# Differential attention's scores on one Trainium2 core: from 128-row products per map to pairs of 64-row products in one four-bank tile

## The chip, the cores and the metric

The kernel runs on one core of one Trainium2 chip. The metric is the device time of one execution in microseconds. Before the change it is 2376.85 us, the median of three runs (2373.96 to 2377.68).

## The reference

A two-layer decoder trunk on x of 1024 tokens by 1024 channels, float32. Layer 0 mixes tokens with gated linear attention, layer 1 with differential attention; each mixer is followed by a SwiGLU, with RMS norms ahead and residual sums behind. The change is in the differential attention alone, whose core is:

```
lam = exp(sum(lam_q1 * lam_k1)) - exp(sum(lam_q2 * lam_k2)) + lambda_init
for blk in range(S // Q_BLOCK):
    s = einsum('bhcqd,bhckd->bhcqk', qb, kb) * scale
    s = where(kpos[None, :] <= qpos[:, None], s, -inf)
    p = softmax(s, axis=-1)
    a = p[:, :, 0] - lam * p[:, :, 1]
    outs.append(einsum('bhqk,bhkv->bhqv', a, vb))
```

There are 8 heads, two maps per head (index c), 64 channels per map, and blocks of 128 query rows. Values have 128 channels per head.

## The kernel before, in words

Activations lie transposed, channels on the partitions, tokens in two halves of 512. Products run with operands in the format fp32r, and an fp32 number is split into a rounded high part and a low part; `mm3` (lines 145 to 148) makes one exact product of three: high by high, high by low, low by high. All projections and both SwiGLU layers use it.

The attention stage is in the second half of `trunk_kernel`, from line 1127 on. For a head n and a half s of the queries, `qstep` and `kstep` project 128 channels (two maps of 64) into a PSUM bank of pool A and split the result. To get by with two products per score bank, they lay the parts so that the contraction has 128 rows: for map m, `kk` holds the high part of K in rows 0 to 63 and the low part in rows 64 to 127; `qh` holds the high part of Q twice, in both halves; `ql` holds the low part of Q in rows 0 to 63, and zeros, written once by POOL, in rows 64 to 127.

`scores(i)` (lines 1196 to 1225) treats the 128 query rows of chunk i, whose score width is W = 128 (i + 1) columns, that is one bank of up to 512 columns for i below 4 and two for i of 4 to 7. For each map it takes a tile of two banks from pool S (two such tiles), makes the products

```
mm(out, qh[:, o:o + P], kk[:, :w], start=True, stop=False)
mm(out, qlo[:, o:o + P], kk[:, :w], start=False, stop=True)
```

then adds the causal mask to the last 128 columns on VectorE (line 1210), takes the negated row maximum (1212), exponentiates on ScalarE with that maximum as bias and the row sum as second result (1215), inverts the sum (1217), and for map 1 multiplies it by minus lambda (1219). Two more VectorE passes scale the first map's rows and add the second's (1223, 1224). `values(i)` transposes the weights by 128 x 128 blocks (1235), copies them back (1236) and multiplies by the values (1240); `dnorm` normalizes a half of a head.

PSUM has eight banks: two tiles of two for scores, one for the outputs (O), one for transposes and norms (C), two for projections (A). A table of blocks, 16 halves of heads, sets what stands beside what: `merge` lays the projections of later heads and the output projection (`dout_steps`) between the chunks of a half. From this the tile framework's scheduler makes the order of each engine; the engines then run that order strictly, waiting on each other through semaphores.

## Time and profile before

| what | value |
| --- | --- |
| median of three runs | 2376.85 us |
| profiled execution, own time | 2377.06 us |
| profiled execution, span from first to last instruction | 2375.3 us |
| PE (products) busy | 2321.8 us, 98% |
| PEld (weight loads, beside PE) busy | 1934.6 us, 81% |
| DVE (VectorE) busy | 1827.5 us, 77% |
| ACT (ScalarE) busy | 1078.4 us, 45% |
| POOL (GpSimd) busy | 191.3 us, 8% |
| mean granted clock of TensorE | 0.996 |

The products overlap in the pipeline and their recorded ends are modelled, so the busy time of PE is no measure of its rate: what a product costs in a stream is read from the distance between two starts. A product of fp32 operands (transposes and values) shows as two records. The first score product starts at 1166.8 us, the last at 1675.2 us from the span's start.

### The profile page before, as it was taken

The numbers are of one execution on the slowest core, as the hardware profiler recorded it, in microseconds if no ns is written. First come the engines' busy times: TensorE is split into PE (matmuls) and PEld (weight loads), VectorE is DVE, ScalarE is ACT, GpSimd is POOL, SyncE is SP. The second block draws the span as 40 slices with busy tenths as digits, with TensorE's granted clock in tenths as the row PEclk, the third lists the DMA queues.
The fourth block names the chain that finished last, engine by engine and source line by source line (L and its number), as shares of the span: only waits on it lengthen the run. The fifth ranks groups of instructions, "written<-read, shape, count | busy, mean of one in ns | idle before, by whom it ended". The sixth has DMA issues, their size and how long they took to land. (4 is left out here: it accounts for less than half of the span.)

```text
span 2375.3 us, 30798 instructions
## 1 busy us (share of the span) xinstructions
PE 2321.8 (98%) x11682; PEld 1934.6 (81%) x11682; DVE 1827.5 (77%) x3039; ACT 1078.4 (45%) x1741; POOL 191.3 (8%) x194
## 2 busy tenths in 40 slices
PE   8999999999999999999999999999999999999997
PEld 7888888888888887887888878887788888887876
DVE  6988676898666667988877785868996666669887
ACT  6555554544333334334565454646543333334344
POOL 4000000000000000442000000000000000002443
PEclk9999999999999999999999999999999999999999
DMA  5121222113233336442010101110113332246332
GB/s 193 45 89 54 89 80 80 55 50 111 94 101 113 114 99 217 144 158 93 32 36 19 36 19 36 36 36 15 48 58 117 109 107 93 94 160 211 121 123 87
DMA packets 82871, 212.15 MB, mean 89 GB/s; under 512 B 9249, under 2 KB 11425, under 8 KB 82722
## 3 DMA queue, kind: packets, MB, share of 16 engines
q1 hardware_dynamic: 82434, 210.02, 26.9%
q8 instruction: 92, 1.51, 0.3%
q14 instruction: 57, 0.47, 0.1%
q10 hardware_dynamic: 288, 0.16, 0.0%
HBM read 167.14 MB, written 42.99 MB: 88 GB/s over the span
## 5 line engine op out<-in xcount | busy, mean ns | idle before, releaser
L881 POOL TENSOR_TENSOR sums<-wraw 128x256 f32<-128x256 f32 x36 | 29.2, 810 | 2100.0 <-DMA wraw<-in_foutc 1083.5
L935 DVE TENSOR_TENSOR x<-x,psB 128x512 f32<-128x512 f32 (+1 forms) x246 | 162.6, 669 | 31.5 <-PE psB L933 31.1
L142 DVE TENSOR_TENSOR w0l<-wraw,w0h 128x1024 fp32r<-128x1024 f32 (+2 forms) x60 | 68.2, 1136 | 98.9 <-ACT w0h L141 98.9
L1215 ACT ACTIVATE p<-sp,mx 128x128 f32<-128x128 f32 (+7 forms) x128 | 94.5, 741 | 82.1 <-DVE mx L1212 79.0
L740 PE MATMUL psB<-hl,w0h 128*128 128x512 f32 x320 | 124.5, 389 | 0.0
L739 PE MATMUL psB<-hh,w0h 128*128 128x512 f32 x320 | 124.5, 389 | 0.0
L741 PE MATMUL psB<-hh,w0l 128*128 128x512 f32 x320 | 124.5, 389 | 0.0
L141 ACT CAST w0h<-wraw 128x1024 fp32r<-128x1024 f32 (+2 forms) x60 | 58.9, 982 | 134.0 <-PE psB L740 112.1
L141 ACT CAST w2h<-wraw 128x1024 fp32r<-128x1024 f32 (+2 forms) x58 | 56.8, 980 | 116.9 <-PE psB L740 86.8
L142 DVE TENSOR_TENSOR w3h<-wraw,w3h 128x512 fp32r<-128x512 f32 x40 | 27.6, 691 | 97.7 <-ACT w3h L141 97.7
L223 DVE TENSOR_TENSOR x<-x,psA 128x512 f32<-128x512 f32 x108 | 73.4, 683 | 33.0 <-PE psA L148 31.5
L1212 DVE TENSOR_REDUCE mx<-sp 128x1 f32<-128x128 f32 (+7 forms) x128 | 94.5, 750 | 1.4
L141 ACT CAST w3h<-wraw 128x512 fp32r<-128x512 f32 x42 | 26.1, 620 | 132.0 <-DMA wraw<-in_fin 131.9
L1240 PE MATMUL psO<-aT,vd 128*128 128x128 f32 x576 | 82.1, 281 | 1.6 <-ACT aT L1236 1.4
L1240 PEld LDWEIGHTS psO<-aT,vd 128*128 128x128 f32 x576 | 72.3, 192 | 12.8 <-ACT aT L1236 11.1
L1207 PE MATMUL sp<-kk,qh 128*128 128x512 f32 (+2 forms) x192 | 69.5, 366 | 2.6 <-ACT p L1215 1.8
L740 PEld LDWEIGHTS psB<-hl,w0h 128*128 128x128 f32 x320 | 60.1, 188 | 12.5
L739 PEld LDWEIGHTS psB<-hh,w0h 128*128 128x128 f32 x320 | 60.1, 188 | 12.5
L741 PEld LDWEIGHTS psB<-hh,w0l 128*128 128x128 f32 x320 | 60.1, 188 | 12.4
L141 ACT CAST w1h<-wraw 128x1024 fp32r<-128x1024 f32 (+1 forms) x44 | 45.5, 1035 | 51.9 <-DVE wraw L711 40.7
L142 DVE TENSOR_TENSOR w2l<-wraw,w2h 128x1024 fp32r<-128x1024 f32 (+2 forms) x58 | 66.7, 1150 | 0.3
L142 DVE TENSOR_TENSOR w1l<-wraw,w1h 128x1024 fp32r<-128x1024 f32 (+1 forms) x44 | 52.8, 1200 | 17.6 <-ACT w1h L141 16.7
(737 smaller groups left out, 7774.6 us busy)
## 6 DMA issues: line engine op xcount, KB each, us to landing
wraw<-in_fin SPq DMA_DIRECT2D x88, 512.0 KB, 3.6
stash<-e SPq DMA_DIRECT2D x108, 256.0 KB, 4.0
hl<-stash SPq DMA_DIRECT2D x80, 256.0 KB, 4.4
wraw<-in_foutc SPq DMA_DIRECT2D x40, 512.0 KB, 3.6
wraw<-in_gin SPq DMA_DIRECT2D x32, 512.0 KB, 3.5
stash<-raw SPq DMA_DIRECT2D x40, 256.0 KB, 4.0
wraw<-in_gv SPq DMA_DIRECT2D x16, 512.0 KB, 3.6
wraw<-in_gout SPq DMA_DIRECT2D x16, 512.0 KB, 3.5
```

The source lines that it names most:

```text
L141: ins = nc.scalar.copy(out=hi, in_=src)
L142: nc.vector.tensor_tensor(out=lo, in0=src, in1=hi.bitcast(F32), op=ALU.subtract)
L223: nc.vector.tensor_tensor(out=xt[m][s], in0=xt[m][s], in1=ps, op=ALU.add)
L739: mm(ps, ah, bh, start=s, stop=False, skip_group_check=cont)
L740: mm(ps, ah, bl, start=False, stop=False, skip_group_check=cont)
L741: mm(ps, al, bh, start=False, stop=i == KH - 1, skip_group_check=cont)
L881: op(out=s1, in0=a21, in1=a22, op=ALU.add)
L935: tt(out=xt[i + o][s][:, c], in0=xt[i + o][s][:, c], in1=ps, op=ALU.add)
L1207: mm(out, qh[:, o:o + P], kk[:, :w], start=True, stop=False)
L1212: nc.vector.reduce_max(out=mx, in_=sp[:, :W], axis=AX.X, negate=True)
L1215: nc.scalar.activation(out=p[:, :W], in_=sp[:, :W], func=AF.Exp, bias=mx, accum_out=sm)
L1240: mm(c["op"][:, o:o + P], tl["v", n // 2][:, j, v * P:(v + 1) * P], aT[:, j * P:(j + 1) * P], start=j == 0, stop=j == i)
```

## The change

Q and K are split once for both maps, with 128 rows each: rows 0 to 63 are map 0, rows 64 to 127 map 1. A score bank is made of three products of 64 rows per map (high by high, high by low, low by high), issued as pairs, map 0 and map 1 one behind the other, each map into its own two banks of a tile of four banks; pool S has one such tile. The products of a chunk are kept in program order and given a higher priority. Scores are made with the sign turned round, so that mask and row minimum are one VectorE instruction over the whole width, which writes the masked scores back; the exponential turns the sign. The row sums of both maps lie in one tile of two columns, inverted together and multiplied by (1, minus lambda) together. The tile p1 gets a second buffer. The output projection of the last heads takes its four borrowed banks from the one tile. The core of the diff:

```diff
-        psum(pc, ("S", 2), ("O", 1), ("C", 1), ("A", 2))
-        ql = [[ap.tile([P, HT], F32R, name=f"ql{i}_{m}") for m in range(2)] for i in range(2)]
-        for i in range(2):
-            for m in range(2):
-                nc.gpsimd.memset(ql[i][m][64:128, :].bitcast(F32), 0.0)
+        psum(pc, ("S", 1), ("O", 1), ("C", 1), ("A", 2))
-        scale = 64 ** -0.5
+        scale = -64 ** -0.5
+        cmask = ap.tile([P, S], F32, name="cmask")
+        nc.gpsimd.memset(cmask, 0.0)
+        nc.gpsimd.affine_select(out=cmask[:, S - P:], in_=cmask[:, S - P:], pattern=[[-1, P]], base=0,
+                                channel_multiplier=1, compare_op=ALU.is_ge, fill=1e30)
...
-                for m in range(2):
-                    src = ps[64 * m:64 * m + 64, :]
-                    hi = ap.tile([P, HT], F32R, name=f"qh{m}", bufs=2)
-                    nc.scalar.mul(hi[0:64, :], src, scale)
-                    nc.scalar.mul(hi[64:128, :], src, scale)
-                    nc.vector.scalar_tensor_tensor(out=ql[s][m][0:64, :], in0=src, scalar=scale,
-                                                   in1=hi[0:64, :].bitcast(F32), op0=ALU.mult, op1=ALU.subtract)
+                hi, lo = [ap.tile([P, HT], F32R, name=f"q{x}", bufs=2) for x in "hl"]
+                nc.scalar.mul(hi, ps, scale)
+                nc.vector.scalar_tensor_tensor(out=lo, in0=ps, scalar=scale, in1=hi.bitcast(F32), op0=ALU.mult,
+                                               op1=ALU.subtract)
...
-                for m in range(2):
-                    src = ps[64 * m:64 * m + 64, :]
-                    kk = ap.tile([P, HT], F32R, name=f"kk{m}", bufs=3)
-                    nc.scalar.copy(out=kk[0:64, :], in_=src)
-                    nc.vector.tensor_tensor(out=kk[64:128, :], in0=src, in1=kk[0:64, :].bitcast(F32),
-                                            op=ALU.subtract)
+                hi, lo = [ap.tile([P, HT], F32R, name=f"k{x}", bufs=3) for x in "hl"]
+                split(hi, lo, ps)
...
-                for m in range(2):
-                    qh, qlo = tl["q", n, s, m]
-                    sp = PS["S"].tile([P, S], F32, name="sp")
+                both = PS["S"].tile([P, 2 * S], F32, name="sp")
+                sps = both[:, :S], both[:, S:]
+                rows = slice(0, 64), slice(64, 128)
+                with tc.high_priority(200):
                     for b in range((W + HT - 1) // HT):
                         w = min(HT, W - b * HT)
-                        kk = tl["k", n, b, m]
-                        out = sp[:, b * HT:b * HT + w]
-                        mm(out, qh[:, o:o + P], kk[:, :w], start=True, stop=False)
-                        mm(out, qlo[:, o:o + P], kk[:, :w], start=False, stop=True)
-                    diag = sp[:, W - P:W]
-                    nc.vector.tensor_tensor(out=diag, in0=diag, in1=cmask, op=ALU.add)
+                        kh, klo = tl["k", n, b]
+                        for x, (q, k) in enumerate(((qh, kh), (qh, klo), (qlo, kh))):
+                            for m in range(2):
+                                ins = mm(sps[m][:, b * HT:b * HT + w], q[rows[m], o:o + P], k[rows[m], :w],
+                                         start=x == 0, stop=x == 2)
+                                if (b, x, m) != (0, 0, 0):
+                                    tc.keep_in_program_order(ins)
+                for m in range(2):
+                    sp = sps[m]
                     mx = ap.tile([P, 1], F32, name="mx", bufs=4)
-                    nc.vector.reduce_max(out=mx, in_=sp[:, :W], axis=AX.X, negate=True)
-                    p = ap.tile([P, S], F32, name=f"p{m}", bufs=2 - m)
-                    sm = ap.tile([P, 1], F32, name="sm", bufs=6)
-                    nc.scalar.activation(out=p[:, :W], in_=sp[:, :W], func=AF.Exp, bias=mx,
-                                         accum_out=sm)
-                    nc.vector.reciprocal(out=sm, in_=sm)
-                    if m == 1:
-                        nc.vector.tensor_tensor(out=sm, in0=sm, in1=neglam, op=ALU.mult)
+                    nc.vector.tensor_tensor_reduce(out=sp[:, :W], in0=sp[:, :W], in1=cmask[:, S - W:], scale=1.0,
+                                                   scalar=1e30, op0=ALU.add, op1=ALU.min, accum_out=mx)
+                    p = ap.tile([P, S], F32, name=f"p{m}", bufs=2)
+                    nc.scalar.activation(out=p[:, :W], in_=sp[:, :W], func=AF.Exp, scale=-1.0, bias=mx,
+                                         accum_out=sm[:, m:m + 1])
+                nc.vector.reciprocal(out=sm, in_=sm)
+                nc.vector.tensor_tensor(out=sm, in0=lam, in1=sm, op=ALU.mult)
```

Since the change also moves instructions, three places of the order follow. In it "x2" means two instructions of one line in a row. Line 1205 of the change is the score product, 1234 and 1239 are the transposes and value products (1235 and 1240 before), 144 to 146 the projections (146 to 148 before).

PE, the chunk of 768 columns (i = 5) of a head in the middle of the stage; before:

```order
L1235 MATMUL psC<-ident,p_11430 128x128 x4
L1207 MATMUL sp<-kk_10834,qh_11070 128x512
L1208 MATMUL sp<-kk_10834,ql_0_9631 128x512
L1207 MATMUL sp<-kk_11147,qh_11070 128x256
L1208 MATMUL sp<-kk_11147,ql_0_9631 128x256
L1207 MATMUL sp<-kk_10837,qh_11074 128x512
L1208 MATMUL sp<-kk_10837,ql_1_9632 128x512
L1207 MATMUL sp<-kk_11150,qh_11074 128x256
L1240 MATMUL psO<-aT,vd 128x128 x4
L1208 MATMUL sp<-kk_11150,ql_1_9632 128x256
```

and with the change, in the next head:

```order
L145 MATMUL psA<-hl_0_9522,w3h 128x512
L1205 MATMUL sp<-kh,qh 128x512 x2
L1205 MATMUL sp<-kl,qh 128x512 x2
L1205 MATMUL sp<-kh,ql 128x512 x2
L1205 MATMUL sp<-kh,qh 128x256 x2
L1205 MATMUL sp<-kl,qh 128x256 x2
L1205 MATMUL sp<-kh,ql 128x256 x2
L166 MATMUL psC<-sq,onesr 128x512
```

Eight score products, into which value products were mixed, have become twelve of half the rows, in six pairs without a break. So it is in 60 of the 64 chunks; in four of the 128-column chunks one to four projections stand between the first pair and the other two.

PE, the end of the stage, from the last score products of head 7's second half (1024 columns) to the first chunks of its first half (128 and 256 columns); before:

```order
L1208 MATMUL sp<-kk_14390,ql_1_9632 128x512
L147 MATMUL psA<-dol_14500,w3h 128x512
L148 MATMUL psA<-doh_14499,w3l 128x512
L1235 MATMUL psC<-ident,p_14554 128x128 x4
L1207 MATMUL sp<-kk_14356,qh_14661 128x128
L1208 MATMUL sp<-kk_14356,ql_0_9629 128x128
L146 MATMUL psA<-doh_14499,w3h 128x512
L1235 MATMUL psC<-ident,p_14554 128x128 x3
L1240 MATMUL psO<-aT,vd 128x128 x7
L147 MATMUL psA<-dol_14500,w3h 128x512
L148 MATMUL psA<-doh_14499,w3l 128x512
L1207 MATMUL sp<-kk_14359,qh_14665 128x128
```

and with the change:

```order
L1205 MATMUL sp<-kh,qh 128x512 x2
L1205 MATMUL sp<-kl,qh 128x512 x2
L1205 MATMUL sp<-kh,ql 128x512 x2
L1234 MATMUL psC<-ident,p_14349 128x128 x7
L1239 MATMUL psO<-aT,vd 128x128 x7
L1205 MATMUL sp<-kh,qh 128x128 x2
L1205 MATMUL sp<-kl,qh 128x128 x2
L1205 MATMUL sp<-kh,ql 128x128 x2
L1234 MATMUL psC<-ident,p_14392 128x128 x7
L1205 MATMUL sp<-kh,qh 128x256 x2
L1205 MATMUL sp<-kl,qh 128x256 x2
L1205 MATMUL sp<-kh,ql 128x256 x2
```

Between the chunk of 1024 columns and the first one of 128 stood two projections and four transposes, with the second map's products for later; now seven transposes and seven value products stand there, and both maps' products follow together.

DVE, the chunk of 1024 columns in head 1 (line 223 before, 221 now, adds the output projection to x); before:

```order
L1210 TENSOR_TENSOR sp<-sp,cmask 128x128
L1212 TENSOR_REDUCE mx<-sp 128x1
L1210 TENSOR_TENSOR sp<-sp,cmask 128x128
L223 TENSOR_TENSOR x_0_82<-x_0_82,psA 128x512
L1212 TENSOR_REDUCE mx<-sp 128x1
L1217 RECIPROCAL sm<-sm 128x1
L223 TENSOR_TENSOR x_0_84<-x_0_84,psA 128x512
L1223 TENSOR_SCALAR p_10944<-p_10944,sm 128x1024
L1217 RECIPROCAL sm<-sm 128x1
L1219 TENSOR_TENSOR sm<-sm,neglam 128x1
L1224 SCALAR_TENSOR_TENSOR p_10944<-p_10956,sm,p_10944 128x1024
```

and with the change, where line 1213 is the new wide instruction and, as "mx", its small second one:

```order
L1213 ISA sp,mx<-sp,cmask 128x1024
L1213 ISA mx 128x1
L221 TENSOR_TENSOR x_0_79<-x_0_79,psA 128x512
L221 TENSOR_TENSOR x_0_81<-x_0_81,psA 128x512
L1213 ISA sp,mx<-sp,cmask 128x1024
L1213 ISA mx 128x1
L1219 RECIPROCAL sm<-sm 128x2
L1220 TENSOR_TENSOR sm<-lam,sm 128x2
L1222 TENSOR_SCALAR p_10884<-p_10884,sm 128x1024
L1223 SCALAR_TENSOR_TENSOR p_10884<-p_10888,sm,p_10884 128x1024
```

Two mask additions, two reductions, two reciprocals and one multiplication have become two wide and two small instructions, one reciprocal and one multiplication, with two x additions between the two maps.

## Rows read from the trace of the kernel before

**Rows 1.** The page, busy time and instructions by engine; granted clock in 40 slices.

```profile
PE 2321.8 (98%) x11682; PEld 1934.6 (81%) x11682; DVE 1827.5 (77%) x3039; ACT 1078.4 (45%) x1741; POOL 191.3 (8%) x194
...
PEclk9999999999999999999999999999999999999999
```

**Rows 2.** Two stretches: length; busy us of PE, PEld, DVE, ACT, POOL; PE's clock.

```profile
1165.00:1700.00 535.00, 518.99 (x3018) 434.43 (x3017) 405.50 (x838) 299.63 (x602) 0.00 (x0) 1.00 0.10 31
...
1650.00:1700.00 50.00, 42.29 (x212) 32.43 (x211) 44.49 (x93) 30.59 (x63) 0.00 (x0) 0.97 0.13 43
```

**Rows 3.** Who waited for whom, 1165:1700: us, times, longest.

```profile
PEld sp L1207 <- ACT p L1215: 7.7, 20, 0.8
PE sp L1207 <- ACT p L1215: 1.8, 4, 0.6
```

**Rows 4.** PE in order of time, score products: start us, length us, line, shape.

```profile
1317.06 0.34 PE L1208 MATMUL sp<-kk,ql 128*128 128x384 f32 x1
1317.23 0.34 PE L1207 MATMUL sp<-kk,qh 128*128 128x384 f32 x1
...
1331.84 0.39 PE L1208 MATMUL sp<-kk,ql 128*128 128x512 f32 x1
1332.07 0.22 PE L1207 MATMUL sp<-kk,qh 128*128 128x128 f32 x1
1332.13 0.27 PE L1208 MATMUL sp<-kk,ql 128*128 128x128 f32 x1
1332.24 0.45 PE L1207 MATMUL sp<-kk,qh 128*128 128x512 f32 x1
1332.53 0.39 PE L1208 MATMUL sp<-kk,ql 128*128 128x512 f32 x1
...
1564.67 0.28 PE L1207 MATMUL sp<-kk,qh 128*128 128x256 f32 x1
1564.79 0.28 PE L1208 MATMUL sp<-kk,ql 128*128 128x256 f32 x1
```

**Rows 5.** PE in order of time, around a block of line 481.

```profile
220.59 0.39 PE L148 MATMUL psA<-hh,w1l 128*128 128x512 f32 x1
220.91 0.68 PE L481 MATMUL psB<-u 128*64 128x64 f32 x8
221.52 0.50 PE L146 MATMUL psA<-oh,w2h 128*128 128x512 f32 x1
221.85 0.40 PE L147 MATMUL psA<-ol,w2h 128*128 128x512 f32 x1
```

**Rows 6.** Weight loads (PEld) in order of time, same stretch.

```profile
220.37 0.19 PEld L148 LDWEIGHTS psA<-hh,w1l 128*128 128x128 f32 x1
220.91 0.54 PEld L481 LDWEIGHTS psB<-u 128*64 128x64 f32 x8 [0.35 <-issue]
...
221.62 0.19 PEld L147 LDWEIGHTS psA<-ol,w2h 128*128 128x128 f32 x1
```

**Rows 7.** Groups by shape, 1165:1690, 1024-wide minimum pass and exponential: busy, mean ns, idle.

```profile
L1212 DVE TENSOR_REDUCE mx<-sp 128x1 f32<-128x1024 f32 x16 | 19.5, 1218 | 0.3
...
L1215 ACT ACTIVATE p<-sp,mx 128x1024 f32<-128x1024 f32 x16 | 17.9, 1117 | 16.9 <-DVE mx L1212 15.7 <-DVE sm L1217 1.2
```

**Rows 8.** PE in order of time, a run of value products.

```profile
1658.44 1.73 PE L1240 MATMUL psO<-aT,vd 128*128 128x128 f32 x14
```

**Rows 9.** Groups by line over the span, DVE in the attention: count, busy us, mean ns.

```profile
L1210 DVE TENSOR_TENSOR sp<-sp,cmask 128x128 f32<-128x128 f32 x128 | 36.7, 293 | 30.2 <-PE sp L1208 29.5
L1166 DVE TENSOR_TENSOR kk<-psA,kk 64x512 fp32r<-64x512 f32 x32 | 22.1, 689 | 8.0 <-ACT kk L1165 7.1
L1153 DVE SCALAR_TENSOR_TENSOR ql<-psA,qh 64x512 fp32r<-64x512 f32 x32 | 21.9, 685 | 9.4 <-ACT qh L1152 8.3
L1217 DVE RECIPROCAL sm<-sm 128x1 f32<-128x1 f32 x128 | 19.8, 159 | 12.5 <-ACT p L1215 11.5
```

**Rows 10.** Groups by shape, DVE, 1650:1700.

```profile
L1210 DVE TENSOR_TENSOR sp<-sp,cmask 128x128 f32<-128x128 f32 x10 | 2.9, 288 | 0.2 <-PE sp L1208 0.2
```

More of the change, by code (lines that the diff above doesn't have):

```diff
@@ L68, in trunk_kernel @@
     onesr = const.tile([P, P], F32R, name="onesr")
-    cmask = const.tile([P, P], F32, name="cmask")
+    lam = const.tile([P, 2], F32, name="lam")
     vec = const.tile([P, 48], F32, name="vec")
-    neglam = const.tile([P, 1], F32, name="neglam")
     gdiff = const.tile([P, 1], F32, name="gdiff")
@@ L89, in trunk_kernel @@
                             compare_op=ALU.is_equal, fill=0.0)
-    nc.vector.memset(cmask, 0.0)
-    nc.gpsimd.affine_select(out=cmask, in_=cmask, pattern=[[-1, P]], base=0, channel_multiplier=1,
-                            compare_op=ALU.is_ge, fill=-1e30)
     dots = const.tile([P, 2], F32, name="dots")
@@ L103, in lam_consts @@
         nc.scalar.activation(out=dots, in_=dots, func=AF.Exp)
+        neglam = lam[:, 1:2]
+        nc.vector.memset(lam, 1.0)
         nc.vector.tensor_tensor(out=neglam, in0=dots[:, 1:2], in1=dots[:, 0:1], op=ALU.subtract)
@@ L1147, in qstep @@
                 proj_half(cq["w"], s, ps)
[L1148 to L1155 removed]
+                hi, lo = [ap.tile([P, HT], F32R, name=f"q{x}", bufs=2) for x in "hl"]
+                nc.scalar.mul(hi, ps, scale)
+                nc.vector.scalar_tensor_tensor(out=lo, in0=ps, scalar=scale, in1=hi.bitcast(F32), op0=ALU.mult,
+                                               op1=ALU.subtract)
+                tl["q", n, s] = (hi, lo)
             def kstep(s):
@@ L1161, in kstep @@
                 proj_half(ck["w"], s, ps)
-                for m in range(2):
-                    src = ps[64 * m:64 * m + 64, :]
-                    kk = ap.tile([P, HT], F32R, name=f"kk{m}", bufs=3)
-                    nc.scalar.copy(out=kk[0:64, :], in_=src)
-                    nc.vector.tensor_tensor(out=kk[64:128, :], in0=src, in1=kk[0:64, :].bitcast(F32),
-                                            op=ALU.subtract)
-                    tl["k", n, s, m] = kk
+                hi, lo = [ap.tile([P, HT], F32R, name=f"k{x}", bufs=3) for x in "hl"]
+                split(hi, lo, ps)
+                tl["k", n, s] = (hi, lo)
             def vstep(t):
@@ L1198, in scores @@
                 o = (i % CPH) * P
-                sums = []
-                for m in range(2):
-                    qh, qlo = tl["q", n, s, m]
-                    sp = PS["S"].tile([P, S], F32, name="sp")
+                sm = ap.tile([P, 2], F32, name="sm", bufs=3)
+                qh, qlo = tl["q", n, s]
+                both = PS["S"].tile([P, 2 * S], F32, name="sp")
+                sps = both[:, :S], both[:, S:]
+                rows = slice(0, 64), slice(64, 128)
+                with tc.high_priority(200):
@@ L1220, in scores @@
                     c["p", i, m] = p
-                    sums.append(sm)
+                nc.vector.reciprocal(out=sm, in_=sm)
+                nc.vector.tensor_tensor(out=sm, in0=lam, in1=sm, op=ALU.mult)
                 p0, p1 = c["p", i, 0], c["p", i, 1]
-                nc.vector.tensor_scalar(out=p0[:, :W], in0=p0[:, :W], scalar1=sums[0], scalar2=None, op0=ALU.mult)
-                nc.vector.scalar_tensor_tensor(out=p0[:, :W], in0=p1[:, :W], scalar=sums[1], in1=p0[:, :W],
+                nc.vector.tensor_scalar(out=p0[:, :W], in0=p0[:, :W], scalar1=sm[:, 0:1], scalar2=None, op0=ALU.mult)
@@ L1225, in scores @@
+                nc.vector.scalar_tensor_tensor(out=p0[:, :W], in0=p1[:, :W], scalar=sm[:, 1:2], in1=p0[:, :W],
                                                op0=ALU.mult, op1=ALU.add)
@@ L1271, in one @@
                 if len(ns) > 2 and m in (2, 3, 4, 5):
-                    if m % 2 == 0:
-                        wout["ps"] = PS["S"].tile([P, S], F32, name="sp")
-                    ps = wout["ps"][:, m % 2 * HT:(m % 2 + 1) * HT]
+                    if m == 2:
+                        wout["ps"] = PS["S"].tile([P, 2 * S], F32, name="sp")
+                    ps = wout["ps"][:, (m - 2) * HT:(m - 1) * HT]
                 out_half([wout[n] for n in ns], [tl["on", n, s] for n in ns], s, m, ps)
```

1 line of the change is left out of this document (removed).

## The prediction

> **What bounds the kernel now.** I read the page's busy shares first: the product engine (PE) is busy for 98% of the span and its granted clock shows the highest digit in every slice [rows 1]. The stage that the change touches, differential attention, lies between 1165 and 1700 us. Two stretches of it are read next [rows 2]: over the whole stage PE is busy 519.0 of 535 us and VectorE (DVE) 405.5, so PE's 16 idle us are all that a faster DVE could win; half of them (50 - 42.3 = 7.7) lie in the last 50 us, where DVE itself is busy 44.5 of 50. Then the waits: in the stage the score products waited 7.7 + 1.8 = 9.5 us, 24 times, for an exponential to give a score tile free [rows 3]. The reader is to see that in this stage nearly every nanosecond of PE is on the path to the end, and that DVE is on it only at the end of the stage. So the forecast is a sum over PE.
>
> **The products.** Before, a score bank takes four products of 128 rows (two maps, lines 1207 and 1208); after, three pairs of 64-row products. Start-to-start times give a product's price: 512 columns 0.23 us (1331.84 to 1332.07), 384 columns 0.175 (1317.06 to 1317.23), 256 columns 0.12 (1564.67 to 1564.79); two of 128 columns take 0.17 and delay the next by 0.06, so 0.115 each [rows 4]. A head has six 512-column score banks and two of each smaller width: 6 x 0.23 + 2 x (0.175 + 0.12 + 0.115) = 2.2 us for one product of each. Before: 4 x 2.2 x 8 heads = 70.4 us. After, if the two of a pair run at the same time: 3 x 2.2 x 8 = 52.8. If they run one after the other: 6 x 2.2 x 8 = 105.6. The trace holds no 64-row product, so these are the ends: 17.6 us won, or 35.2 lost. I take the won end, because the two use different halves of the rows and write different banks, and the order keeps every pair together. [...]
>
> **The change of array shape.** The kernel has one place where products of another shape stand among full ones: line 481, blocks of eight with 64 columns, in the first layer. From the product before the block to the second one after it pass 221.85 - 220.59 = 1.26 us [rows 5], and it waited for nothing else (issue) [rows 6]. Two 512-column products are 0.46 of that. The block's 0.68 us is seven spacings and one product's length; with a length near 0.22, that of a 128-column score product [rows 4], the spacings are 0.46, and one more is 0.06. So 0.28 us are lost even before the block's own first load is counted. Behind the block the first product took 0.33 rather than 0.23, because its weights were not loaded ahead: its successor's load starts 0.10 behind its own start, at 221.62, while in the plain stream a load starts with the product before it (220.37) [rows 6]. A block of 64-row products with 128-column weights pays the same 0.10 at its entry, so I take 0.38 us per block. The order shows 64 chunks, of which four have their first pair parted from the rest by projections: 68 blocks, 68 x 0.38 = 25.8 us. Between full-shape score products and projections nothing of the kind is paid: the step from 1332.07 on runs at the plain spacing [rows 4]. The ends: nothing, if a change in rows is free; 25.8, if it is like that change in columns. I take 25.8, from the one measured place. [...]
>
> **The score tile.** Before, two tiles of two banks; after, one of four, so the next chunk's products wait for both maps' exponentials. That removes the 24 waits inside a chunk [rows 3]: -9.5 us; at worst they stay (0). In exchange the chain for one 1024-wide chunk is two reductions of 1.22 and one exponential of 1.12, 3.56 us, plus handovers [rows 7]. What covers it is PE's work up to the next chunk. In the tail, between the last chunk of head 7's second half and the first chunk of its first half, stand seven transposes and seven value products, two records of 0.11 us each (1.73 us for 14 records less a last one's length of 0.28, over 13) [rows 8]: 14 x 0.22 = 3.1 us. So about 1 us is lost there; elsewhere projections lie between. But DVE now puts two x additions between the two maps' minima of a chunk in the middle heads, and whatever stands there lengthens the chain. I charge 3 us for all chunks, between 0 and 10.
>
> **DVE and ScalarE.** 128 additions of the mask go (0.293 us each, 36.7 us), 64 reciprocals of 0.159 (10.2), and half of the 32 + 32 splits of Q and K (32 x 0.69 = 22) [rows 9]. The mask now rides in the wide pass. The trace has no such pass; I price it like the reduction over the same width, which also reads the score bank once (0 more; at most the mask addition again). Each minimum also has a small second instruction; between nothing and a reciprocal's 0.16, I take 0.16 x 128 = 20. DVE falls by some 49 of 405 us, the multiplication by lambda stays one per chunk. All of that is hidden under PE, except in the last 50 us: there the ten mask additions of five chunks go (2.9 us) [rows 10] with some five reciprocals (0.8), and ten small instructions come (1.6): 2.1 us, of which I count 2. Were DVE the bound elsewhere too, the gain would be larger; its 405 of 535 us speak against that. ScalarE loses 64 of its 96 Q and K conversions, all hidden; POOL's four memsets of ql give way to one of the mask and its select, before the first score, while POOL stands idle in the whole stage (0.00 us) [rows 2].
>
> **Sum.** -17.6 + 25.8 - 9.5 + 3 - 2 = -0.3 us. The profiled execution took 2377.06 us (span 2375.3), 0.2 us over the median of the three runs, so the forecast is 2376.8 us: no change. What a measurement of this kernel can tell from no change is about 0.2%, 4.8 us.
>
> **Rivals.**
> - *The change of shape costs little.* Then the 25.8 is near 0: 2376.8 - 25.8 = 2351, or 2364 if half is paid. For it: what was measured at line 481 is a change of columns; here the weights keep 128 columns and only rows are halved, and each half could be loaded while the other is at work. [...] Faster.
> - *The pairs run one after the other* (the slower side). Place: line 1205, 288 pairs; price 35.2 + 17.6 = 52.8 us over the forecast, 2430; if the shape change is free as well, 2404. It decides early: a second product that starts 0.02 us late on the mean already costs 288 x 0.02 = 5.8 us, more than the 0.2%; wholly serial pairs are late by 0.18 on the mean (52.8 / 288). For it: nothing in the trace runs at once on PE; every start is one product's columns behind the last. Against it: different rows, different banks, neighbours in the queue.
> - *Weight loads bound the pairs.* Two loads per pair rather than one per product. A 128-column product with its load is held to 0.115 us [rows 4], so a pair to 0.23 if loads go one at a time. Then every pair narrower than 512 pays 0.23: 3 x 12 x 0.23 x 8 = 66 us rather than 52.8, 13 us more, 2390. For it: that floor is in the rows. Against it: the two loads go to different rows.
> - That the change doesn't do what it says is excluded by the order: every pair stands together (x2), 68 blocks.
>
> **Chances.** Forecast 0.39 (its own range 2370 to 2385: 0.02 faster, 0.20 within 0.2%, 0.17 slower, since of its unknowns more lie above than below). Shape change cheap 0.38, all of it faster: 2351 to 2368. Loads bound 0.10, slower. One after the other 0.13, slower. So faster 0.40, same 0.20, slower 0.40. The range reaches down to the cheap shape change with nothing charged for the score tile (2351 - 3 = 2348) and up to the loads' rival with 9 rather than 3 us for it (2396); the serial rival is left out.
>
> **What would show it.** Right: line 1205 as pairs whose starts are a few ns apart and whose pairs are 0.23 us apart at 512 columns; around each block about 0.1 us before and 0.2 behind; PE's stage as long as before, with DVE some 50 us less busy in it. The first rival: the projection behind a block starts one spacing after the last pair, and the stage is 15 to 25 us shorter. The serial rival: starts 0.2 us apart within a pair. The loads' rival: pairs of 128 columns 0.23 us apart. The S tile: waits of line 1205 for line 1216's exponentials of more than 10 us in all would make the forecast too low, and so would a wide pass on DVE clearly longer than the reduction at its width.

## The result and the profile after

The changed kernel took 2404.91 us (median of four runs, 2404.51 to 2405.52), the kernel before 2377.23 in the same comparison: a ratio of 1.0123, 95% interval 1.011 to 1.0135. That is 27.7 us slower, outside the range, where no change was forecast.

The page, busy shares and granted clock by slice (before: [rows 1]):

```profile
PE 2334.8 (97%) x11874; PEld 1923.0 (80%) x11874; DVE 1783.6 (74%) x2943; ACT 1040.8 (43%) x1677; POOL 190.5 (8%) x191
...
PEclk9999999999999999999999999999899999999999
```

The two stretches of [rows 2], same columns:

```profile
1165.00:1700.00 535.00, 507.75 (x3082) 404.94 (x3082) 338.12 (x692) 249.76 (x513) 0.00 (x0) 0.98 0.10 31
1650.00:1700.00 50.00, 37.93 (x191) 27.52 (x190) 35.62 (x76) 26.45 (x58) 0.00 (x0) 0.83 0.13 43
```

In this stretch DVE is busy 67 us less than before and PE still has 11 us more without work. Part of the 67 is only shift, since the changed kernel has less of the stage behind it at 1700 us; over the whole of attention, between the marks of the next paragraph, DVE's work fell by 44.7 us, from 490.7 to 446.0. So relieving DVE did not relieve PE. In the last 50 us PE worked 4.4 us less than before, at a mean clock of 0.83 rather than 0.97.

Where the time went follows from three marks. Attention starts behind the first layer's last product, at 1129.4 us before and 1125.8 after, and ends with the second layer's first feed-forward product, at 1758.45 and 1785.83: 31.0 us longer. (The first layer's end differs by 3.6 us; in the profiled execution before, the granted clock was 0.50 twice there, from 102.1 and from 242.0 us, for 6.8 us in all, of which up to half is lost.) Counted from the start of attention, the copy of the finished values of the 13th of 16 half-heads is 15.1 us late, that of the last 24.4. So half of it is a steady loss, and half arises behind the 13th half-head, in the last 151 us of the stage before, which are 167 now.

PE in order of time, around a chunk of two banks (start us, length us, line, shape; x2 is a pair):

```profile
1331.24 0.39 PE L146 MATMUL psA<-doh,w2l 128*128 128x512 f32 x1
1331.56 0.50 PE L1205 MATMUL sp<-kh,qh 64*128 64x512 f32 x2
1331.89 0.39 PE L1205 MATMUL sp<-kl,qh 64*128 64x512 f32 x2
1332.12 0.39 PE L1205 MATMUL sp<-kh,ql 64*128 64x512 f32 x2
1332.35 0.28 PE L1205 MATMUL sp<-kh,qh 64*128 64x256 f32 x2
1332.47 0.28 PE L1205 MATMUL sp<-kl,qh 64*128 64x256 f32 x2
1332.59 0.28 PE L1205 MATMUL sp<-kh,ql 64*128 64x256 f32 x2
1332.81 0.50 PE L144 MATMUL psA<-doh,w1h 128*128 128x512 f32 x1
1333.14 0.40 PE L145 MATMUL psA<-dol,w1h 128*128 128x512 f32 x1
```

This is as forecast: pairs stand 0.23 us apart at 512 columns and 0.12 at 256, so the two of a pair run at once; over all 288 pairs the second product starts 5.6 ns behind the first on the mean. The change of shape shows too, at each block (a run of 64-row products with no full-size product in it): 0.32 instead of 0.23 into the block, 0.33 instead of 0.23 for its first pair, 0.22 instead of 0.12 behind the last pair, 0.33 instead of 0.23 for the first product after it. Together that is 0.39 us more than plain spacings, where 0.38 was forecast.

What was not forecast are the waits. The score products for an exponential, same stretch and columns as [rows 3]:

```profile
PE sp L1205 <- ACT p L1216: 4.4, 3, 2.1
PEld sp L1205 <- ACT p L1216: 17.7, 41, 2.3
```

That is 22.1 us, 44 times, where there had been 9.5 us, 24 times, and where I expected 3. Not all of it is lost time: 17.7 of the 22.1 (and 7.7 of the 9.5) are idle times of the weight loads, beside which PE may still be at work. PE's own waits of all kinds, in 1120:1790, sum to 30.8 us against 16.6; of the 14.2 more, 2.6 stand before score products and 4.6 before transposes that wait for the combined probabilities (line 1223), the end of the same chain. The softmax of one chunk shows why. DVE first, then ACT, in order of time:

```profile
1322.98 0.82 DVE L1213 CUSTOM_DVE_ANT_0 sp<-sp,cmask 128x640 f32<-128x640 f32 x1
1323.73 0.14 DVE L1213 DVE_READ_ACCUMULATOR2_ANT mx<- 128x1 f32 x1
1324.96 0.69 DVE L221 TENSOR_TENSOR x<-x,psA 128x512 f32<-128x512 f32 x1 [1.09 <-PE psA L146]
1329.60 0.83 DVE L1213 CUSTOM_DVE_ANT_0 sp<-sp,cmask 128x640 f32<-128x640 f32 x1 [3.96 <-ACT p L1216]
```

```profile
1327.82 0.59 ACT L1178 COPY vd<-psA 128x512 f32<-128x512 f32 x1 [6.53 <-PE psA L146]
1328.30 0.49 ACT L1235 COPY aT<-psC 128x384 f32<-128x384 f32 x1
1328.67 0.81 ACT L1216 ACTIVATE p<-sp,mx 128x640 f32<-128x640 f32 x1
1329.36 0.21 ACT L1216 ACTIVATION_READ_ACCUMULATOR p<-sp,mx 128x1 f32 x1
1330.53 0.79 ACT L1216 ACTIVATE p<-sp,mx 128x640 f32<-128x640 f32 x1 [0.96 <-DVE mx L1213]
```

Two things are to be seen. **The second map's minimum waits for the first map's exponential**: 1329.60 is the end of the exponential (1329.36 + 0.21) and a handover. The pass writes the score tile in place, the exponential reads the other half of the same tile, and the program orders the two by the tile. So the softmax of a chunk runs minimum, exponential, minimum, exponential, with no overlap. The order in which the program stands shows the same on DVE (its waits in brackets, one chunk):

```
1452 L1213 ISA sp,mx<-sp,cmask 128x256 [waits PE_49]
1453 L1213 ISA mx 128x1
1455 L1213 ISA sp,mx<-sp,cmask 128x256 [waits Activation_49]
1456 L1213 ISA mx 128x1
```

**The first exponential stands in ACT's queue behind a copy** that waits 6.53 us for a value projection (L1178). The raised priority took the score products ahead of that projection on PE, but not the exponential ahead of the copy on ACT, so the finished scores lie there from 1323.9 to 1328.7.

Measured over all 64 chunks, from the trace: in 64 of 64 the second minimum starts behind the first exponential's end (before: 25), and from the first minimum's start to the second exponential's end pass 6.16 us on the mean (before: 3.92, or 4.72 from the start of the mask addition, which the minimum now includes). For all that time the only score tile is taken. The second cause shows there too: between the first minimum and its exponential lie 2.66 us on the mean, where there were 0.81.

The tail, PE in order of time:

```profile
1667.99 0.51 PE L1205 MATMUL sp<-kh,qh 64*128 64x512 f32 x2 [2.07 <-ACT p L1216]
1668.33 0.60 PE L1205 MATMUL sp<-kl,qh 64*128 64x512 f32 x2
1668.72 0.63 PE L1205 MATMUL sp<-kh,ql 64*128 64x512 f32 x2
1669.15 0.64 PE L1205 MATMUL sp<-kh,qh 64*128 64x512 f32 x2
...
1676.08 0.33 PE L1205 MATMUL sp<-kh,qh 64*128 64x128 f32 x2 [1.26 <-ACT p L1216]
...
1678.68 1.09 PE L1234 MATMUL psC<-ident,p 128*128 128x128 f32 x4 [2.05 <-DVE p L1223]
```

Here only transposes and value products stand between two chunks, and PE waits for the rest of the chain. Behind the wait of 2.07 us the spacing of 512-column pairs goes from 0.23 to 0.43 us: the granted clock fell to 0.50 (at 1668.35 us; the mean over the stretch 1669 to 1670 is 0.50). The clock rows show 20.5 us at 0.50 in the last 120 us of attention, where before there were 3.4; at most half of it is lost, 10.2 against 1.7 us, since PE also stands idle in some of it.

The groups of DVE by line:

```profile
L1213 DVE CUSTOM_DVE_ANT_0 sp<-sp,cmask 128x128 f32<-128x128 f32 (+7 forms) x128 | 97.6, 762 | 77.2 <-ACT p L1216 72.8 <-PE sp L1205 4.1
L1213 DVE DVE_READ_ACCUMULATOR2_ANT mx<- 128x1 f32 x128 | 18.2, 142 | 0.0
L1219 DVE RECIPROCAL sm<-sm 128x2 f32<-128x2 f32 x64 | 10.5, 164 | 37.7 <-ACT p L1216 37.6
```

The wide pass costs 762 ns on the mean (the reduction took 750 over the same widths) and its second instruction 142, as priced. The first row's idle time is the new wait.

### The profile page after: what moved, and what is told of

Its sections match the earlier page's. It is cut to its first block, busy times and chain, and to the rows that moved or that the text cites. A ratio compares the mean times of both kernels' runs of the same rounds, so it can differ in the third digit from the quotient of the medians.

```text
span 2402.8 us, 31010 instructions
## 1 busy us (share of the span) xinstructions
PE 2334.8 (97%) x11874; PEld 1923.0 (80%) x11874; DVE 1783.6 (74%) x2943; ACT 1040.8 (43%) x1677; POOL 190.5 (8%) x191
## 3 DMA queue, kind: packets, MB, share of 16 engines
q1 hardware_dynamic: 82434, 210.02, 26.5%
## 5 line engine op out<-in xcount | busy, mean ns | idle before, releaser
L1213 DVE CUSTOM_DVE_ANT_0 sp<-sp,cmask 128x128 f32<-128x128 f32 (+7 forms) x128 | 97.6, 762 | 77.2 <-ACT p L1216 72.8
L140 DVE TENSOR_TENSOR w3h<-wraw,w3h 128x512 fp32r<-128x512 f32 x40 | 27.7, 692 | 98.5 <-ACT w3h L139 98.5
L221 DVE TENSOR_TENSOR x<-x,psA 128x512 f32<-128x512 f32 x108 | 73.7, 685 | 28.8 <-PE psA L146 27.8
L1235 ACT COPY aT<-psC 128x512 f32<-128x512 f32 (+2 forms) x96 | 46.0, 480 | 71.6 <-PE psC L1234 71.1
L140 DVE TENSOR_TENSOR w1l<-wraw,w1h 128x1024 fp32r<-128x1024 f32 (+1 forms) x44 | 52.9, 1201 | 17.4 <-ACT w1h L139 16.9
```

The source lines that it names most:

```text
L140: nc.vector.tensor_tensor(out=lo, in0=src, in1=hi.bitcast(F32), op=ALU.subtract)
L221: nc.vector.tensor_tensor(out=xt[m][s], in0=xt[m][s], in1=ps, op=ALU.add)
L1213: nc.vector.tensor_tensor_reduce(out=sp[:, :W], in0=sp[:, :W], in1=cmask[:, S - W:], scale=1.0, scalar=1e30, op0=ALU.add, op1=ALU.min, acc ...
```

## The experiments

Each run beside the kernel before on the same chip (2374.7 to 2375.9 us in the five comparisons):

| run | us | ratio to before, 95% | what it is |
| --- | --- | --- | --- |
| rows128 | 2406.19 | 1.0133 (1.0119 to 1.0146) | change without pairs: 128-row products |
| extra_full | 2411.11 | 1.0158 (1.0143 to 1.0172) | 32 more blocks |
| extra_half | 2408.62 | 1.0145 (1.0131 to 1.0158) | its control |
| fused_only | 2380.77 | 1.0027 (1.0017 to 1.0037) | fused pass, joint factors |
| tile1 | 2416.73 | 1.0175 (1.0160 to 1.0190) | fused_only, one tile |
| prio2 | 2398.21 | 1.0095 (1.0080 to 1.0111) | rows128, two tiles |
| no_prio | 2411.71 | 1.0146 (1.0129 to 1.0163) | change without priority |
| narrow_double | 2425.50 | 1.0212 (1.0197 to 1.0228) | change, two small tiles |
| fused_split | 2379.03 | 1.0021 (1.0012 to 1.0030) | fused_only, factors apart |
| after_split | 2393.47 | 1.0080 (1.0066 to 1.0094) | change, factors apart |
| prio_only | 2391.76 | 1.0068 (1.0054 to 1.0082) | fused_only, priority |
| order2 | 2382.14 | 1.0030 (1.0018 to 1.0042) | prio2 without priority |
| rows128_split | 2406.04 | 1.0133 (1.0117 to 1.0148) | rows128, factors apart |
| apart | 2405.06 | 1.0125 (1.0111 to 1.0139) | change, map by map |
| shared_lo | 2378.58 | 1.0016 (1.0007 to 1.0025) | before, low parts shared |
| b_half | 2395.67 | 1.0086 (1.0071 to 1.0101) | before, 64 small blocks |
| pairs2n | 2396.96 | 1.0086 (1.0069 to 1.0102) | order2 with pairs |
| after_p1 | 2405.98 | 1.0125 (1.0110 to 1.0140) | change, one buffer p1 |

**The frame without pairs.** By frame I mean what is left of the change when the pairs are taken out: one tile, fused pass, joint factors, priority and fixed order. rows128:

```diff
-for x, (q, k) in enumerate(((qh, kh), (qh, klo), (qlo, kh))):
+for x in range(2):
     for m in range(2):
-        ins = mm(..., q[rows[m], o:o + P], k[rows[m], :w], start=x == 0, stop=x == 2)
+        ins = mm(..., tl["q", n, s, m][x][:, o:o + P], tl["k", n, b, m][:, :w], start=x == 0, stop=x == 1)
```

> The changed kernel, but with score products of 128 rows (two per map and bank, as before; the low parts of Q of both maps share one tile, one buffer of the second map's probabilities): one tile of four banks, the fused mask and minimum, the joint factors, the priority and the fixed order stay. It has no change of array shape and no pairs. Theory (the 27.7 us are about 14 won by the pairs, 26 paid for the 68 changes of shape, and some 15 paid for waits on the one score tile and in the tail): 2405 - 26 + 14 = 2393 us, 2388 to 2398. Rival A (the score tile costs nothing, pairs and their changes of shape cost all): 2377 us, 2373 to 2381. Rival B (changes of shape cost next to nothing, the single tile costs all): 2405 + 14 = 2419 us.

2406.19 us: as slow as the changed kernel, without one pair or change of shape. My theory then, which made these two cost 12 us net, missed by 13 us on one side, rival B by 13 on the other, rival A by 29: the frame costs more than I thought, and pairs and shape nearly cancel. (rows128 also keeps the 64 conversions on ScalarE and the 32 splits on DVE of Q and K that the pairs save, so these are part of what cancels.)

**More blocks.** extra_full, and extra_half, which takes rows 0 to 63 of qh and kh:

```diff
+if b == 1:
+    tc.keep_in_program_order(mm(sps[0][:, HT:HT + P], qh[:, o:o + P], kh[:, :P], start=True, stop=True))
```

> The changed kernel plus one more product of 128 rows by 128 columns between the pairs of the first and of the second bank, in the 32 chunks that have two banks; it writes where the second bank's pair writes over it. So 32 more blocks of 64-row products, and 32 more products of about 0.1 us. To be read against extra_half, which has the same product with 64 rows. Theory (a block costs about 0.39 us): extra_full - extra_half = 32 x 0.39 = 12.5 us, 10 to 15; extra_full itself 2405 + 3 + 12.5 = 2420 us. Rival A (a block costs all, 41 us / 68 = 0.6 us): 19 us. Rival B (a change of shape costs next to nothing): under 3 us.

> The changed kernel plus one more product of 64 rows by 128 columns between the pairs of the first and of the second bank in the 32 chunks that have two banks; it changes no shape. All theories: 32 x 0.06 to 0.12 us = 2 to 4 us over the changed kernel, 2407 to 2409 us.

2411.11 and 2408.62 us: 2.5 us for 32 blocks, with intervals of some 3.5 us on each side. By the number this is rival B, and the theory's 10 to 15 us failed. In the traces attention grew by 4.0 us from extra_half to extra_full, while PE's waits in 1120:1790 shrank from 33.1 to 26.5 us: much of what a block costs went into time in which PE waited anyway. So in the changed kernel one more block costs about 0.1 us of time, whatever it costs on PE.

**The fused pass.** fused_only, and fused_split, which has a reciprocal for each map as before:

```diff
-nc.vector.tensor_tensor(out=diag, in0=diag, in1=cmask, op=ALU.add)
-nc.vector.reduce_max(out=mx, in_=sp[:, :W], axis=AX.X, negate=True)
+nc.vector.tensor_tensor_reduce(out=sp[:, :W], in0=sp[:, :W], in1=cmask[:, S - W:], ..., op1=ALU.min, accum_out=mx)
```

> The kernel before with the fused mask and minimum and the joint factors alone: two score tiles of two banks, 128-row products, no priority, no fixed order (the low parts of Q of both maps share one tile). Theory (the loss lies in the shape and in the single tile, the fused pass is no longer than the reduction was and takes 128 mask additions off DVE): 2 to 6 us less than before, 2371 to 2375 us. Rival (the wide pass with its second small instruction sits on the path from score to exponential and delays PE): 2377 us or more, up to 2390.

> fused_only with the factors of the two maps apart again (a reciprocal for each map, the second times minus lambda), so that the first map's probabilities can be scaled while the second map's exponential still runs. Theory J (the joint factors lengthen the way from score to combined probabilities by about one scaling pass, 0.5 to 1 us a chunk, and that is what made fused_only 5 us slower): 2370 to 2376 us. Rival F (the fused pass with its second small instruction does it): 2379 to 2384 us, like fused_only.

2380.77 and 2379.03 us, both somewhat slower than before, each in the range of the rival that blames the fused pass. But these variants need room for the wide mask, so the low parts of Q of both maps share a tile; shared_lo has that alone:

> The kernel before with the low parts of Q of both maps in one tile (rows 0 to 63 and 64 to 127, and K of the second map with its high part in the lower rows) as in my variants with 128-row products; nothing else. Theory (the fused pass is what makes fused_split 4 us slower): 2374 to 2377 us, as before. Rival (the shared tile does it): 2378 to 2381 us.

2378.58 us: the shared tile makes 3.4 of it, and what is left for the fused pass with factors apart, 0.5 us, is within the intervals. It gains nothing and costs nothing here. Every variant with 128-row products that has the wide mask shares that tile; that it costs 3.4 us in each of them was not measured.

**One tile or two, priority or none.** tile1 gives fused_only one tile of four banks; prio2 gives rows128 two tiles of two; prio_only and order2 set the priority and the fixed order alone; no_prio takes the priority from the changed kernel. The tile of tile1, and the line that prio_only has more than fused_only and prio2 more than order2:

```diff
-sp = PS["S"].tile([P, S], F32, name="sp")
+both = PS["S"].tile([P, 2 * S], F32, name="sp")
+sp = both[:, m * S:(m + 1) * S]
...
+with tc.high_priority(200):
```

> fused_only with one score tile of four banks for both maps in place of two tiles of two banks; 128-row products, no priority, no fixed order. Theory (the single tile is what costs: the next chunk's first product waits for the second map's exponential rather than the first's): 2400 to 2408 us, like rows128. Rival P (the priority puts score products into the queue ahead of projections that could have run, and the tile is harmless): 2379 to 2386 us, like fused_only.

> rows128 with two score tiles of two banks again: priority and fixed order of both maps' products stay, the single tile goes. Theory (the single tile costs): 2380 to 2388 us if the second tile is enough, though the fixed order makes every chunk ask for both tiles at its start, so up to 2395. Rival P (the priority and the fixed order cost): 2400 to 2408 us, no better than rows128.

> fused_only with the raised priority around each map's score products; two tiles, no fixed order, so the second map's products need not stand with the first's. Theory O (what costs is that a chunk's products ask for both maps' banks at one place in the queue): 2378 to 2386 us, like fused_only. Rival P (the priority puts products into the queue too early): 2393 to 2402 us, like prio2.

> prio2 without the priority: two tiles of two banks, 128-row products of both maps in one fixed order. Theory O: 2395 to 2408 us, no better than prio2 (2398). Rival P: 2378 to 2386 us.

> The changed kernel without the raised priority of the score products. Theory (the single tile costs, priority does little): 2400 to 2412 us. Rival P: 2380 to 2392 us.

The tile by itself costs 36 us (tile1 2416.73, fused_only 2380.77), more than the theory's range allowed. The waits of the score products for an exponential, 1120:1790, in fused_only and then in tile1:

```profile
PE sp L1209 <- ACT p L1215: 3.1, 8, 0.6
PEld sp L1209 <- ACT p L1215: 11.0, 28, 1.0
```

```profile
PE sp L1210 <- ACT p L1216: 14.2, 15, 2.3
PEld sp L1210 <- ACT p L1216: 32.0, 56, 2.5
```

14.1 us against 46.2. With two tiles, the fixed order costs nothing (fused_only 2380.77, order2 2382.14), and the priority costs 11 us without the order (prio_only 2391.76) and 16 with it (prio2 2398.21). So rival P holds there in kind, though both times lie just below its ranges, and theory O fell. The same waits in order2 and then in prio2:

```profile
PE sp L1211 <- ACT p L1222: 4.4, 7, 1.4
PEld sp L1211 <- ACT p L1222: 10.2, 19, 1.5
```

```profile
PE sp L1211 <- ACT p L1222: 6.0, 14, 1.4
PEld sp L1211 <- ACT p L1222: 21.8, 54, 1.5
```

14.6 us against 27.8. From the first minimum to the second exponential's end a chunk takes 3.31 us in order2, 6.14 in prio2 and 10.41 in prio_only. What grows is the time from a minimum to its exponential: 0.4 us for the first map and 0.8 for the second in order2, 0.9 and 3.3 in prio2, 4.3 and 4.6 in prio_only. The scores come earlier, the exponentials do not. Where priority and order are there already, one tile costs 8 us on top (rows128 against prio2). The serial softmax goes with the tile: the second minimum starts behind the first exponential in 64 of 64 chunks of tile1, rows128, no_prio and every other run with one tile, in 6 of order2, 11 of prio2, 10 of fused_only. With one tile the priority helps a little (no_prio 2411.71, 6.8 us slower than the changed kernel, at the edge of the intervals): without it the 68 blocks fall into 88 pieces. There the stretch from first minimum to second exponential is only 3.86 us, no longer than before, and yet the score products wait 23.8 us for exponentials. So one tile is dear without a long stretch too. That the next chunk can't start on the half of the tile that is done is the likely reason; no run isolates it.

**Half of the chunks double-buffered.** narrow_double:

```diff
+if W <= HT:
+    both = PS["S"].tile([P, S], F32, name="sp"); sps = both[:, :HT], both[:, HT:]
+else:
+    sps = [PS["S"].tile([P, S], F32, name="sp") for _ in range(2)]
```

> The changed kernel, but the 32 chunks of up to 512 columns keep both maps in one tile of two banks, of which there are two; wide chunks take both. So two narrow chunks can be in flight. Theory (the single tile costs): half of the chunks no longer wait, 10 us less at least, 2388 to 2397 us. Rival P: 2401 to 2408 us. In both the tail (heads 7 with wide chunks) stays as it is.

2425.50 us, a miss for theory and rival. The order shows why it can't decide: with two tiles the first product of a wide chunk breaks away, and there are 127 blocks rather than 68. The second minimum waits in 32 of 64 chunks, the narrow ones, whose maps share a tile.

**Factors apart.** after_split and rows128_split undo the joint reciprocal (the new lines stand in the loop over the maps, behind the exponential):

```diff
-nc.vector.reciprocal(out=sm, in_=sm)
-nc.vector.tensor_tensor(out=sm, in0=lam, in1=sm, op=ALU.mult)
+    nc.vector.reciprocal(out=sm, in_=sm)
+    if m == 1:
+        nc.vector.tensor_tensor(out=sm, in0=sm, in1=neglam, op=ALU.mult)
```

> The changed kernel with the factors of the two maps apart again, else unchanged. Theory J: 4 to 8 us less than the changed kernel, 2397 to 2401 us. Rival F: 2402 to 2408 us.

> rows128 with the factors of the two maps apart, to be read against after_split (2393.5), which is the same frame with pairs of 64 rows. Theory H (pairs win 14, 68 changes of shape cost 24, and in the changed kernel most of the difference was hidden under waits for the softmax; with a shorter chain it shows): 2383 to 2389 us, some 5 to 10 below after_split. Rival Z (pairs and shape really are worth nothing together): 2392 to 2397 us.

2393.47 us: 11.4 less than the changed kernel; 2406.04: nothing. Both lie outside all the ranges above, and in fused_split it was 1.7. The combined probabilities come 0.4 to 0.9 us earlier in all three, counted from the first minimum. Why only one of them turns that into 11 us stays open; the scheduler also places other instructions anew. It also leaves open what pairs and shape are worth: with joint factors the kernel with pairs is 1.3 us faster than the one without (2404.91 and 2406.19), with factors apart 12.6 (2393.47 and 2406.04).

**One buffer for the second map's probabilities**, as rows128 and rows128_split have it:

```diff
-p = ap.tile([P, S], F32, name=f"p{m}", bufs=2)
+p = ap.tile([P, S], F32, name=f"p{m}", bufs=2 - m)
```

> The changed kernel with one buffer rather than two for the second map's probabilities, as rows128 and rows128_split have it. If that buffer is what held those two up: 2413 to 2420 us, and the pairs with their shape are then worth more than rows128 tells. If not: 2403 to 2408 us.

2405.98 us: that buffer does nothing here, so rows128 is a fair comparison in this.

**The change of shape alone, and the pairs alone.** b_half:

```diff
+if m == 0 and b == 0:
+    mm(out[:, :P], qh[0:64, o:o + P], kk[0:64, :P], start=True, stop=True)
 mm(out, qh[:, o:o + P], kk[:, :w], start=True, stop=False)
```

> The kernel before plus, in each of the 64 chunks, one more product of 64 rows by 128 columns ahead of map 0's products, written over by them: 64 blocks of one 64-row product each, two tiles, no priority. Theory (a change of shape costs about 0.27 to 0.39 us a block on PE, and PE is what bounds the stage of the kernel before): 64 x (0.3 + 0.1) = 26 us over before, 2393 to 2406. Rival (a change of shape is hidden or cheap): 64 x 0.06 to 0.11 = 4 to 7 us, 2378 to 2384.

pairs2n, against the changed kernel:

```diff
-both = PS["S"].tile([P, 2 * S], F32, name="sp")
-sps = both[:, :S], both[:, S:]
+sps = [PS["S"].tile([P, S], F32, name="sp") for _ in range(2)]
...
-with tc.high_priority(200):
...
-            for m in range(2):
+            for m in (1, 0):
```

> order2 with pairs of 64-row products (Q and K split once) in place of 128-row products: two tiles, no priority. Without the single tile the chunks' first products stand apart more often: 118 blocks. Theory (pairs win 14, a block costs about 0.35): -14 + 118 x 0.35 = +27 us over order2 (2382), 2400 to 2414. Rival (a change of shape is cheap): 2368 to 2380.

b_half took 2395.67 us, 20.2 over before; PE in it:

```profile
1403.18 0.39 PE L148 MATMUL psA<-doh,w4l 128*128 128x512 f32 x1
1403.50 0.32 PE L1208 MATMUL sp<-kk,qh 64*128 64x128 f32 x1
1403.75 0.50 PE L1209 MATMUL sp<-kk,qh 128*128 128x512 f32 x1
1404.09 0.40 PE L1210 MATMUL sp<-kk,ql 128*128 128x512 f32 x1
```

From 1403.18 to 1404.09 pass 0.91 us, against 0.52 by plain spacings: 0.39 again, and so in most of the 64 blocks (median 0.40). Of the time, 64 products of 0.06 make 3.8 us, and 16.4 / 64 = 0.26 us a block reach the end. pairs2n took 2396.96 us, below the range of its theory and far above the rival's. With 118 blocks it is 14.8 us slower than order2: with some 14 us won by the pairs, (14.8 + 14) / 118 = 0.24 us a block, or up to 0.30 with 17.6 us won and 3.4 us in order2 from its shared tile. The two agree.

**Map by map.** apart exchanges the loops:

```diff
-for x, (q, k) in enumerate(((qh, kh), (qh, klo), (qlo, kh))):
-    for m in range(2):
+for m in range(2):
+    for x, (q, k) in enumerate(((qh, kh), (qh, klo), (qlo, kh))):
```

> The changed kernel with the three products of map 0 ahead of the three of map 1 in each bank, so that neighbours use the same rows; operands, shapes and blocks stay. If the two products of a pair ran at the same time (theory), PE's score slots grow from 53 to 88 (each bank six products in a row, of which only the middle two are of different rows and can overlap) to 106 us, and the time by 20 to 50: 2425 to 2455 us. Rival (no gain in time from the overlap, since the chain hides it): 2404 to 2412 us.

2405.06 us, no change, and not because the chain hides it:

```profile
1330.30 0.51 PE L1205 MATMUL sp<-kh,qh 64*128 64x512 f32 x2
1330.63 0.40 PE L1205 MATMUL sp<-kl,qh 64*128 64x512 f32 x2
1330.86 0.40 PE L1205 MATMUL sp<-kh,ql 64*128 64x512 f32 x2
```

The queue holds three products of one map and then three of the other, yet they ran in twos, 10 ns apart. So the edit did not part the pairs, and it can't tell what the pairs are worth. See the last section.

## Why the prediction was wrong

- **The pairs, -17.6.** That the two of a pair run at once was an estimate, which no run had shown; it was right (5.6 ns apart on the mean), and the size too as far as it is known. By the spacings of [rows 4] and of the rows above, all score products take 66.9 us before, if a 128-column product counts 0.06 us, or the prediction's 70.4, if the delay of the product behind it is counted too, and 52.9 after: 14 to 17.6 us won.
- **The change of shape, +25.8.** The price on PE, carried over from columns to rows as an estimate, was right (0.39 for 0.38 a block). But only about two thirds of it reach the end where little is waited for (b_half, pairs2n): 68 x 0.26 = 18 us, and in the changed kernel itself, by extra_full, a third of it or less. With the pairs that is +4 net at most, where +8 was forecast (25.8 - 17.6). Measured directly, pairs and shape together come to about +2 us (the changed kernel against rows128 less 3.4 for the shared tile, known to some 5), but to -9 with factors apart, so their net is not settled.
- **The score tile, "-9.5" and "+3".** This is the step that failed. I wrote that "the chain for one 1024-wide chunk is two reductions of 1.22 and one exponential of 1.12", and charged "3 us for all chunks, between 0 and 10". The chain is two minima and two exponentials, one after the other, because the program orders the pass on one half of the tile behind the exponential that reads the other half. For the eight 1024-wide chunks it takes 5.37 us on the mean, from the first minimum's start to the second exponential's end, not 3.56. Then the raised priority, which I priced at nothing, lets finished scores lie in the tile until their exponentials come up: over all chunks 6.16 us, where it was 4.72 with the mask. The waits of [rows 3] grew from 9.5 to 22.1 us instead of going (and of the 9.5 only 1.8 had been PE's own, so it is not shown that 9.5 were there to win), and PE's time at a granted clock of 0.50 in the tail, 20.5 us against 3.4, costs up to 8.5 us more than before. The cover in the tail was overestimated too: in the trace before a transpose is one record, not two, and starts 0.11 us behind the one ahead of it (1656.83 to 1656.94), so seven of them and seven value products are 2.3 us, not 3.1. One tile, priority and order together, measured without pairs: 2406.19 - 2380.77 = 25 us, where -6.5 stood in the sum. The tile alone is shown to cost (36 us in tile1); how much of that is the serial softmax and how much the next chunk's later start, no run separates.
- **DVE and ScalarE, -2.** Prices right (762 and 142 ns), gain absent: DVE's saving, forecast at some 49 us and hidden, was 44.7 and hidden, and in the last 50 us PE waits for the chain, not for DVE's load (35.6 of 50). The joint factors, forecast as some five reciprocals fewer, put the scaling of the first map behind the second exponential; undoing them gives 11 us in the changed kernel and none in rows128.
- **Rivals.** None named this way. The slower side was given to serial pairs and to weight loads, which the rows exclude: starts 5.6 ns apart on the mean within a pair, and 128-column pairs 0.11 us apart (1676.25 to 1676.36), not 0.23. The cheap change of shape is excluded on PE by the 0.39. The line in the prediction that waits of over 10 us on line 1205 would make it too low was the right alarm, with the wrong chance behind it.

These parts overlap (a wait can hide a change of shape, and the clock fell beside a wait), so they don't add up to 27.7 to the microsecond. As an account of PE's time in the two traces, the 31.0 us of attention are 14 to 17.6 less for the products, 26.5 more for 68 blocks of 0.39, at most 8.5 more for the clock, and for the waits what is left, 10 to 14; but without the blocks the waits grow, and rows128 is no faster. Not tried: writing the fused pass out to another tile than the one it reads, which might take away the serial softmax and free the score tile early; and two tiles with whole blocks, which the order did not give. No version that was run beats the kernel before.

## What to carry to other kernels

In this program a buffer is released and ordered by tile, not by bank: before two buffers are joined into one, and above all when a reader is turned into an in-place writer, list for each instruction which others touch the same tile, and look in the program's order for a new wait. Work that is moved ahead on one engine only fills its buffer earlier; if its consumers' queues are not moved with it, the buffer is held longer (16 us here, with two tiles). A block of 64-row products among full ones cost about 0.39 us on PE and 0.26 of time where PE was the bound, and pairs in place of 128-row products save 0.23 us per 512-column bank, so by these prices a block of one bank doesn't pay for itself.

## What the hardware showed that was not expected

- In apart, products on the two row halves did not wait for each other in the queue: the fourth product in order started 10 ns behind the first and 0.33 us ahead of the second, and the time (2405.06 against 2404.91) goes with the trace. So "run that order strictly", as said of the engines ahead, is not true of PE's products on different rows there, and pinning the pairs side by side was not needed for the overlap.
- A change in rows alone, with 128 columns kept, costs at three of its four places what the change in columns at line 481 cost by the prediction's reading of [rows 5]: 0.09 us into the block in both, 0.10 behind it against 0.09, 0.10 for the first product after it in both. The fourth, 0.10 for the block's own first pair, can't be read from the merged rows of line 481.
- Beside two waits of PE of about 2 us in the tail the granted clock fell to 0.50: from 0.4 us behind the end of the first and 0.1 us ahead of the end of the second. At 0.50, 512-column pairs stand 0.43 us apart. fused_only, whose PE waits little more than the kernel before (17.6 against 16.6 us in 1120:1790), has 13.6 us at 0.50 in the tail against 3.4 (mean clock 0.86 in 1650:1700 against 0.97), each in the one profiled execution.
